# Which quads of the feed-forward blocks read stored weight sums, and when the sums are made

## The chip, the cores and the metric

The kernel runs on one core of a Trainium2 chip. The metric is the device time of one execution in microseconds, as the median of several runs.

## The reference

Two layers, each a token mixer and a feed-forward network, over 256 tokens of width 2048 in float32. The change touches the feed-forward part, whose work is

```python
def _swiglu(x, w_gate, w_up, w_down):
    h = jax.nn.silu(jnp.einsum('bsd,df->bsf', x, w_gate)) * jnp.einsum('bsd,df->bsf', x, w_up)
    return jnp.einsum('bsf,fd->bsd', h, w_down)

for i in range(DEPTH):
    mix = _hybrid_mixer(x, positions, w_in[i], g_cq[i], g_ckv[i], w_uq[i], w_ukv[i], w_o[i])
    x = _layer_norm(ALPHA * x + mix, ln1_g[i], ln1_b[i])
    ffn = _swiglu(x, w_gate[i], w_up[i], w_down[i])
    x = _layer_norm(ALPHA * x + ffn, ln2_g[i], ln2_b[i])
```

with a hidden width of 5632. The mixer projects x (`w_in`), runs a sparse attention and a latent attention (`w_uq`, `w_ukv`), and projects their outputs with `w_o`.

## The kernel before

**Units and remainders.** A weight tile (a unit) is 128x1024 float32, 512 KB: two k-tiles of 128 rows by 512 columns. SyncE's queue loads it into a tile `raw` (L323). `parts` (L338 to L351) splits it: ScalarE rounds it to `wh`, VectorE subtracts to get the remainder `wl`. TensorE computes a product with three matmuls of 128x512: x's high part with wh, with wl, and x's low part with wh. The tiles have a few buffers each (raw 4, wh and wl 5, and 6 and 2 more of them in the feed-forward part), so a load waits until the split of an earlier unit has read its buffer, and a split until the matmuls have read theirs.

**Blocks and quads.** The 5632 hidden columns are 11 blocks (`fc`, 0 to 10) of 512. Block 0 is computed plainly. For blocks 1 to 10, `gate_up` takes gate and up together, in four quads: quad u has the units u and u+4 of the 8 units of each matrix, which makes a 2x2 product (two token halves, two k halves, two matrices). There are three kinds. A *plain* quad (N) does the 8 products with 4 units. A *wino* quad (S) does 7 products with sums of weight units; it loads three units and, through GpSimd's queue, a sum of two (`load_sum`, L324 to L330: a load and an accumulating load), and VectorE makes three more sums in place (L1050, L1057, L1062) between the splits of its 7 units. A *made* quad (Q) has the same 7 products, but reads the four sums p4 to p7 ready from HBM, as plain loads of `raw`. A product is 6 matmuls. Per block the order of kinds is in `ORDER` and the quad of each in `UNIT` (L1150, L1151): block 1 is NSSS, blocks 2 and 3 SSNS, blocks 4 to 10 SSQS with u = 0 as the Q. VectorE adds the products up in `e` and `g` (L1032), ahead of `silu`.

**Operands.** The 7 products need sums of x's parts, too (`sum_operands`): av (L932), sv (L937), and their high and low parts in `few` or `many`. Those of quads 1 to 3 are made in block 0, those of quad 0 (`first_operands`, twelve VectorE instructions with the remainders of few at L396) in the down half ahead of block `ALLFROM` = 4, the first block that has a Q.

**Down halves.** From block 2 on, `down_half(fc)` ahead of each gate-and-up multiplies two earlier hidden blocks with half of `w_down`'s columns (L1105 to L1107).

**Stored sums.** `presums` (L770) is a generator that runs beside the attention: for each block from `ALLFROM` on, it loads four units into tiles q through GpSimd's queue (L778), which first writes one column from the newest wh, so that the load does not start earlier than that unit (L339); four units later a small GpSimd instruction (gate, L788) waits for the newest wh again, VectorE makes the four sums (L789 to L793), and GpSimd's queue stores them to HBM (L798). `spawn` starts a generator and each finished unit steps it (`tick`). `presums` is spawned behind the projection block TB and makes 7 sets in each layer; `finish(early)` ends it ahead of the output projection's last pass.

**Order.** The instructions of an engine stand in the order in which a scheduler puts the program; `high_priority` pulls some ahead. Each engine and each issuing queue works in its order and waits at the head for what it lacks. The mixer's blocks come as QI0, TA (the latents' block), QI1, TB, KA0 and so on; then `w_o` in four column blocks and a last pass (`last_pass`). `turn("more")` ahead of it closes the attention's pool of tiles and opens the pool of the feed-forward part: the first tile of the new pool waits for all that used the old memory, the stores of q among it.

Of the kernel before, what the change touches and what calls it, by code (L numbers as in the profile page):

```python
# [34 lines left out]
S = 256  # L35
# [26 lines left out]
SOON = 200  # L62
FIRSTD = 2
T2, T2MORE = 4, 6
ALLFROM, EARLY = 4, 0


QI0, TA, QI1, TB, KA0, QA0, VA0, KA1, QA1, VA1 = range(10)
# [14 lines left out]
def hybrid_trunk(ctx: ExitStack, tc: tile.TileContext, x, xt_in, pos, w_in, g_cq, g_ckv, w_uq,  # L83
# [28 lines left out]
    def pt(shape, dt, s, tag=None, bufs=1):  # L112
        assert phase["name"] == "att"
        return phase["pool"].tile(shape, dt, name=nm(s), tag=tag or s, bufs=bufs)
# [423 lines left out]
    def layer(l, xT, norms, last):  # L538
        xk = xlhs(xT)

        def in_chunk(b, before=None, split_t=None):
            n = IN_BLOCKS[b][1]
            return proj([(w_in[b][l, u], range(u * KU, (u + 1) * KU)) for u in range(NKT // KU)], xk, n,
                        before, split_t)
# [222 lines left out]

        ready = {}

        def presums():  # L770

            for fc in range(ALLFROM, NFC):
                u = EARLY

                def load(i, v):
                    d = pt([P, KU * C], F32, "q", bufs=4)
                    not_until_now(d)
                    nc.gpsimd.dma_start(d, w_gu[i][l, fc, v])  # L778
                    return d

                b12, b22 = load(1, u), load(1, u + HALF)
                yield 1
                b11 = load(0, u)
                yield 1
                b21 = load(0, u + HALF)
                yield 4
                gate = pt([P, 1], F32, "gate", bufs=2)
                nc.gpsimd.tensor_tensor(gate, b12[:, 0:1], f(latest["wh"][:, 0:1]), op=ALU.add)  # L788
                nc.vector.tensor_tensor(b12, b12, b22, op=ALU.add)  # L789
                nc.vector.tensor_tensor(b11, b12, b11, op=ALU.add)  # L790
                yield 1
                nc.vector.tensor_tensor(b22, b11, b22, op=ALU.subtract)
                nc.vector.tensor_tensor(b21, b11, b21, op=ALU.add)  # L793
                yield 1
                ready[fc] = {}
                for i, (name, v) in enumerate((("p7", b12), ("p6", b11), ("p5", b22), ("p4", b21))):
                    d = hbm.tile([P, KU * C], F32, name=nm("q"), tag=f"{l}_{fc}_{name}", bufs=1)
                    nc.gpsimd.dma_start(d, v)  # L798
                    ready[fc][name] = d
                    if i % 2:  # L800
                        yield 1
# [24 lines left out]
        ckvT = t4([P, 2, KVL // P, S], F32R, "ckvT")  # L826
        qpT = t4([P, M_HEADS // 2, S], F32, "qpT")
        bias = [pt([P, P * (t + 1)], F32, f"selb{t}") for t in range(NT)]
        o = in_chunk(TA)
        aff(1)  # L830
        p_ta = spawn(ta_post(o))
# [6 lines left out]
        p_tb = spawn(tb_post(o))  # L838
        if l == 0:
            load_x()  # L840
        early = spawn(presums())
        ka, p_ka = dsa_qk(KA0)
        finish(p_tb)
        o = proj([(w_uq[2][l, u], range(u * KU, (u + 1) * KU)) for u in range(QL // P // KU)], cqk, C)
# [54 lines left out]
                        nc.vector.scalar_tensor_tensor(sl, o, by, sl, op0=ALU.mult, op1=ALU.add)  # L899
                then(t)  # L900

        finish(early)
        turn("more")
        gbT = load_gbT(ln1_T[l])
        xT, norms = [], []
# [241 lines left out]
        def finish_hidden():  # L1147
            finish(*[h[2] for h in held])

        ORDER = {1: "NSSS", 2: "SSNS", 3: "SSNS"}  # L1150
        UNIT = {"NSSS": (0, 2, 3, 1), "SSNS": (1, 2, 0, 3), "SSQS": (1, 2, EARLY, 3)}  # L1151

        g = gu(0, 0, lambda: finish(*norms))
        affine(ln1_g[l], ln1_b[l], 0)
        u = gu(1, 0)
# [1 line left out]
        affine(ln1_g[l], ln1_b[l], 1)  # L1157
        spawn_hidden(0, g, u)
        for fc in range(1, NFC):
            order = ORDER.get(fc, "SSQS")  # L1160
            if fc >= FIRSTD:
                down_half(fc)
                finish_hidden()
            g, u = gate_up(fc, [({"N": "plain", "S": "wino", "Q": "made"}[k], v) for k, v in zip(order, UNIT[order])],
                           finish_hidden if fc < FIRSTD else None)
            if fc < FIRSTD:
                for c in range(2, D // C):
                    affine(ln1_g[l], ln1_b[l], c)
            spawn_hidden(fc, g, u)
# [69 lines left out]
```

## Time and profile before

| what | us |
|---|---|
| median of 3 runs (2143.92 to 2145.48) | 2145.45 |
| the profiled execution | 2147.09 |
| its span | 2145.3 |
| TensorE busy | 2129.4 (99%) |
| TensorE's weight loads busy | 1768.9 (82%) |
| VectorE busy | 1850.9 (86%) |
| ScalarE busy | 1311.5 (61%) |
| transfers | 260 GB/s on average |

The span runs from the first to the last instruction; the profiled execution's own time lies some 2 us above it. A busy TensorE is not one at its peak, since matmuls overlap: their starts tell its pace. Layer 1 repeats layer 0 some 1063.7 us later. The feed-forward blocks 1 to 4 of layer 0 lie between 434.78 and 661.05 us, each as a gate-and-up (to 475.69, 538.19, 600.28, 661.05) with a down half behind it. The granted TensorE clock is full in all the stretches below.

### The profile page before, as it was taken

What the parts mean: (1) busy time and instruction counts of PE and PEld (TensorE: products, weight loads), DVE (VectorE), ACT (ScalarE), POOL (GpSimd) and SP (SyncE); (2) the same over time, 40 slices, a digit from 0 to 9 for tenths busy, and PEclk for the clock granted to TensorE, in tenths of its full rate; (3) what the DMA queues carried; (4) which work ended last, traced back from release to release, by engine and by line L of the source; (5) the groups of instructions that cost most, each with busy time, mean ns of one, the idle gap of its engine ahead of it and who ended that gap; (6) DMA issues with size and microseconds to landing.
All of it is one profiled execution on the core that took longest, in us unless ns stands there. A gap on an engine that the chain in (4) does not pass through costs nothing.

```text
span 2145.3 us, 28442 instructions
## 1 busy us (share of the span) xinstructions
PE 2129.4 (99%) x9946; PEld 1768.9 (82%) x9946; DVE 1850.9 (86%) x2343; ACT 1311.5 (61%) x1695; POOL 321.6 (15%) x514
## 2 busy tenths in 40 slices
PE   9999999999999999999999999999999999999997
PEld 7888888888888888888888888888888888888886
DVE  6697776899999999999867976678999999999997
ACT  5555554766566666766655555447666666666773
POOL 0122220021111100110013222201111111110111
PEclk9999999999999999999999999999999999999999
DMA  8677879588888899888657877885897888989984
GB/s 295 216 279 272 310 277 328 175 217 267 239 245 270 286 278 300 269 273 255 216 176 242 298 276 276 315 281 187 245 274 224 256 265 274 288 275 293 286 296 115
DMA packets 161905, 558.21 MB, mean 260 GB/s; under 512 B 18161, under 2 KB 18465, under 8 KB 161121
## 3 DMA queue, kind: packets, MB, share of 16 engines
q1 hardware_dynamic: 111168, 399.69, 52.2%
q0 software_dynamic: 50448, 156.57, 28.4%
q8 instruction: 78, 1.28, 0.2%
q14 instruction: 67, 0.54, 0.1%
q10 hardware_dynamic: 144, 0.13, 0.0%
HBM read 503.37 MB, written 31.46 MB: 249 GB/s over the span
## 4 chain that ended last, share of the span: by engine, by line
PE 86%; DVE 7%; issue 3%; DMA 2%; ACT 1%; POOL 0%; SPq 0%; POOLq 0%; DVEq 0%; ACTq 0%
PE acc L372 8%; PE acc L373 8%; PE acc L374 8%; PE acc L1106 7%; PE acc L1107 7%; PE acc L1105 7%; PE gu_p L996 6%; PE gu_p L993 6%; PE gu_p L995 6%; DVE wl L351 3%; PE gu_c L993 3%; PE gu_c L996 3%; PE gu_c L995 3%; PE tr L392 2%; PE att L993 2%
## 5 line engine op out<-in xcount | busy, mean ns | idle before, releaser
L350 ACT ACTIVATE wh<-raw 128x1024 fp32r<-128x1024 f32 (+1 forms) x918 | 946.6, 1053 | 576.0 <-PE acc L374 142.8
L351 DVE TENSOR_TENSOR wl<-raw,wh 128x1024 fp32r<-128x1024 f32 (+1 forms) x918 | 1084.9, 1213 | 204.4 <-ACT wh L350 202.4
L372 PE MATMUL acc<-wh,xhl 128*128 128x512 f32 (+1 forms) x768 | 303.0, 395 | 0.8 <-ACT wh L350 0.7
L373 PE MATMUL acc<-wl,xhl 128*128 128x512 f32 (+1 forms) x768 | 297.2, 387 | 1.1 <-DVE wl L351 1.1
L374 PE MATMUL acc<-wh,xhl 128*128 128x512 f32 (+1 forms) x768 | 297.5, 388 | 0.0
L1105 PE MATMUL acc<-wh,hT 128*128 128x512 f32 x640 | 250.9, 392 | 0.0
L1106 PE MATMUL acc<-wl,hT 128*128 128x512 f32 x640 | 249.2, 389 | 0.1
L1107 PE MATMUL acc<-wh,hT 128*128 128x512 f32 x640 | 249.3, 390 | 0.0
L372 PEld LDWEIGHTS acc<-wh,xhl 128*128 128x128 f32 x768 | 144.7, 188 | 31.9 <-issue 3.9
L373 PEld LDWEIGHTS acc<-wl,xhl 128*128 128x128 f32 x768 | 144.8, 188 | 28.6 <-DVE wl L351 2.9
L374 PEld LDWEIGHTS acc<-wh,xhl 128*128 128x128 f32 x768 | 144.5, 188 | 27.9
L1106 PEld LDWEIGHTS acc<-wl,hT 128*128 128x128 f32 x640 | 120.2, 188 | 25.3 <-DVE wl L351 1.0
L1107 PEld LDWEIGHTS acc<-wh,hT 128*128 128x128 f32 x640 | 120.1, 188 | 25.1
L1105 PEld LDWEIGHTS acc<-wh,hT 128*128 128x128 f32 x640 | 120.2, 188 | 24.3
L1114 POOL DMA_DIRECT2D x<-d x80 | 67.8, 848 | 482.4 <-ACT d L1113 482.1
L995 PE MATMUL gu_c<-wl,xhl 128*128 128x512 f32 x344 | 134.0, 390 | 0.0
L996 PE MATMUL gu_c<-wh,xhl 128*128 128x512 f32 x344 | 133.8, 389 | 0.0
L993 PE MATMUL gu_c<-wh,xhl 128*128 128x512 f32 x344 | 133.8, 389 | 0.0
L993 PE MATMUL gu_p<-wh,many 128*128 128x512 f32 x240 | 93.4, 389 | 0.0
L995 PE MATMUL gu_p<-wl,many 128*128 128x512 f32 x240 | 93.4, 389 | 0.0
L996 PE MATMUL gu_p<-wh,many 128*128 128x512 f32 x240 | 93.4, 389 | 0.0
L1113 ACT ACTIVATE d<-acc 128x512 f32<-128x512 f32 x80 | 47.8, 597 | 71.5 <-PE acc L1107 70.8
(296 smaller groups left out, 3795.8 us busy)
## 6 DMA issues: line engine op xcount, KB each, us to landing
raw<-in_w_gate_dram SPq DMA_DIRECT2D x176, 512.0 KB, 5.4
raw<-in_w_down_dram SPq DMA_DIRECT2D x176, 512.0 KB, 8.6
raw<-in_w_in_dram SPq DMA_DIRECT2D x144, 512.0 KB, 5.2
sum<-in_w_up_dram POOLq DMA_DIRECT2D x120, 512.0 KB, 7.4
raw<-in_w_up_dram SPq DMA_DIRECT2D x102, 512.0 KB, 5.7
raw<-in_w_o_dram SPq DMA_DIRECT2D x64, 512.0 KB, 5.6
q<-q POOLq DMA_DIRECT2D x56, 512.0 KB, 4.4
raw<-q SPq DMA_DIRECT2D x56, 512.0 KB, 5.9
```

The costliest lines, as they stand in the source:

```text
L350: nc.scalar.activation(wh[:, :n], raw[:, :n], AF.Copy)
L351: nc.vector.tensor_tensor(wl[:, :n], raw[:, :n], f(wh[:, :n]), op=ALU.subtract)
L372: mm(o[t][:, :n], h, a, start=first, stop=False)
L373: mm(o[t][:, :n], h, b, start=False, stop=False)
L374: mm(o[t][:, :n], l, a, start=False, stop=final)
L993: mm(o[name], h, a, start=name not in begun, stop=False)
L995: mm(o[name], h, b, start=False, stop=False)
L996: mm(o[name], l, a, start=False, stop=end)
L1105: mm(o[c][t], h, wh[:, j, :], start=begin, stop=False)
L1106: mm(o[c][t], h, wl[:, j, :], start=False, stop=False)
L1107: mm(o[c][t], lo, wh[:, j, :], start=False, stop=end)
L1114: nc.gpsimd.dma_start(xt[t][:, c * C:(c + 1) * C], d, accum_op=ALU.add)
```

## The change

Blocks 1 to 4 and 6 to 10 get a made quad, block 5 none. Block 1 becomes NSQS, with quad 3 as the Q; blocks 2 and 3 become SSQS like 4 and 6 to 10; block 5 becomes SSSS. `presums` takes a list of (block, quad): 9 sets per layer, of which the first two, (1, 3) and (2, 0), are spawned right behind QI0 and the other seven behind TB as before, with a first wait of three units. `first_operands` moves from the down half ahead of block 4 to that ahead of block 2, with `ALLFROM` = 2.

```diff
-ALLFROM, EARLY = 4, 0
+ORDER = {1: "NSQS", 5: "SSSS"}
+UNIT = {"NSQS": (0, 2, 3, 1), "SSQS": (1, 2, 0, 3), "SSSS": (1, 2, 0, 3)}
+ALLFROM = 2
+
+
+def quads(fc):
+    order = ORDER.get(fc, "SSQS")
+    return list(zip(order, UNIT[order]))
...
-        def presums():
-
-            for fc in range(ALLFROM, NFC):
-                u = EARLY
+        made = [(fc, u) for fc in range(1, NFC) for k, u in quads(fc) if k == "Q"]
+
+        def presums(sets, wait=1):
+
+            yield wait
+            for fc, u in sets:
...
+        early = [spawn(presums(made[:2]))]
         o = in_chunk(TA)
...
-        early = spawn(presums())
+        early.append(spawn(presums(made[2:], 3)))
...
-        finish(early)
+        finish(*early)
...
-        ORDER = {1: "NSSS", 2: "SSNS", 3: "SSNS"}
-        UNIT = {"NSSS": (0, 2, 3, 1), "SSNS": (1, 2, 0, 3), "SSQS": (1, 2, EARLY, 3)}
```

Three places show how the order of instructions moves. The lines of the changed kernel are 10 to 13 higher than those of the kernel before: its L361 is L351, L406 is L396, L945 and L950 are L932 and L937, L977 is L964, L1045 is L1032, L1063, L1070 and L1075 are L1050, L1057 and L1062.

VectorE from block 1's last products into the down half behind it, before: remainders wl of the weights alternate with the adding up of the products in g and e.

```order
L1032 TENSOR_TENSOR e_4512<-e_4512,gu_p_4392 128x512
L351 TENSOR_TENSOR wl_4615<-raw_4612,wh_4614 128x1024
L1032 TENSOR_TENSOR g_4513<-gu_c_4271,e_4512 128x512
L351 TENSOR_TENSOR wl_4633<-raw_4630,wh_4632 128x1024
L1032 TENSOR_TENSOR e_4512<-e_4512,att_4296 128x1024
L351 TENSOR_TENSOR wl_4653<-raw_4650,wh_4652 128x1024
L1032 TENSOR_TENSOR e_4512<-e_4512,gu_p_4414 128x1024
L351 TENSOR_TENSOR wl_4685<-raw_4682,wh_4684 128x1024
L964 TENSOR_TENSOR g_4513<-g_4513,e_4512 128x1024
```

The same place in the changed kernel; wl_4669 and wl_4687 are the down half's first two remainders, wl_4732 its third.

```order
L361 TENSOR_TENSOR wl_4687<-raw_4684,wh_4686 128x1024
L1045 TENSOR_TENSOR e_4566<-e_4566,gu_p_4444 128x512
L406 TENSOR_TENSOR few_4704<-sv_4713,few_4704 128x256
L1045 TENSOR_TENSOR g_4567<-gu_c_4323,e_4566 128x512
L950 TENSOR_TENSOR sv_4717<-av_4702,av_4711 128x256
L1045 TENSOR_TENSOR e_4566<-e_4566,att_4348 128x1024
L945 TENSOR_TENSOR av_4721<-xhl_3751 128x256
L1045 TENSOR_TENSOR e_4566<-e_4566,gu_p_4466 128x1024
L406 TENSOR_TENSOR few_4704<-sv_4717,few_4704 128x256
L977 TENSOR_TENSOR g_4567<-g_4567,e_4566 128x1024
L950 TENSOR_TENSOR sv_4723<-av_4721,sv_4713 128x256
L361 TENSOR_TENSOR wl_4732<-raw_4729,wh_4731 128x1024
```

The down half's first two remainders now stand ahead of the adding up, and six small instructions of `first_operands` among it, ahead of the third remainder.

VectorE in block 5, from the second quad into the third, before: the third quad (raw_6528 to raw_6570, a Q) is seven remainders in a row.

```order
L351 TENSOR_TENSOR wl_6519<-raw_6453,wh_6518 128x1024
L351 TENSOR_TENSOR wl_6535<-raw_6528,wh_6534 128x1024
L351 TENSOR_TENSOR wl_6545<-raw_6530,wh_6544 128x1024
L351 TENSOR_TENSOR wl_6555<-raw_6532,wh_6554 128x1024
L351 TENSOR_TENSOR wl_6573<-raw_6564,wh_6572 128x1024
L351 TENSOR_TENSOR wl_6583<-raw_6566,wh_6582 128x1024
```

The same place in the changed kernel: the third quad is raw_6609 to raw_6613 with sum_6606.

```order
L361 TENSOR_TENSOR wl_6597<-raw_6531,wh_6596 128x1024
L361 TENSOR_TENSOR wl_6626<-raw_6611,wh_6625 128x1024
L361 TENSOR_TENSOR wl_6636<-raw_6613,wh_6635 128x1024
L1063 TENSOR_TENSOR raw_6609<-sum_6606,raw_6609 128x1024
L361 TENSOR_TENSOR wl_6658<-sum_6606,wh_6657 128x1024
L1070 TENSOR_TENSOR raw_6611<-raw_6609,raw_6611 128x1024
L361 TENSOR_TENSOR wl_6647<-raw_6609,wh_6646 128x1024
L1075 TENSOR_TENSOR raw_6613<-raw_6609,raw_6613 128x1024
```

Three sums now stand between its remainders.

TensorE at block 5's end, before: the last product (gu_p, three matmuls for each k-tile) and the first of the down half (acc).

```order
L993 MATMUL gu_p_6439<-wh_6692,many_4186 128x512
L995 MATMUL gu_p_6439<-wl_6693,many_4186 128x512
L996 MATMUL gu_p_6439<-wh_6692,many_4186 128x512
L993 MATMUL gu_p_6439<-wh_6692,many_4186 128x512
L995 MATMUL gu_p_6439<-wl_6693,many_4186 128x512
```

The same place in the changed kernel.

```order
L1006 MATMUL gu_p_6517<-wh_6768,many_4238 128x512
L1118 MATMUL acc_6783<-wh_6787,hT_6257 128x512
L1118 MATMUL acc_6821<-wh_6825,hT_6257 128x512
L1008 MATMUL gu_p_6517<-wl_6769,many_4238 128x512
L1009 MATMUL gu_p_6517<-wh_6768,many_4238 128x512
```

Two matmuls of the down half, which read no remainder, now stand ahead of the one that reads the last product's.

SyncE's queue at the end of the attention, before, with the semaphores waited for (DMASW are GpSimd's transfers, the stores of q among them; raw_3606, raw_3616 and raw_3621 are units of the last pass, the others of `w_o`'s column blocks).

```order
L323 DMA raw_3425<-in_w_o_dram 128x1024 [waits DMAHW7_49,DVE_49]
L323 DMA raw_3606<-in_w_o_dram 128x1024 [waits DMASW3_49,DMASW2_49,DMASW4_49,DMASW1_49,DMASW5_49,DMASW0_49,DMASW6_49,PE_49,DMASW7_49,Activation_49,Pool_49]
L323 DMA raw_3443<-in_w_o_dram 128x1024 [waits DMAHW0_49,DVE_49]
L323 DMA raw_3616<-in_w_o_dram 128x1024
L323 DMA raw_3621<-in_w_o_dram 128x1024
L323 DMA raw_3461<-in_w_o_dram 128x1024 [waits DMAHW1_49,DVE_49]
```

The same place in the changed kernel; raw_3495 and raw_3513 are the units of raw_3443 and raw_3461.

```order
L333 DMA raw_3495<-in_w_o_dram 128x1024 [waits DMAHW0_49,DVE_49]
L333 DMA raw_3658<-in_w_o_dram 128x1024 [waits DMASW3_49,DMASW4_49,DMASW2_49,DMASW5_49,DMASW1_49,DMASW6_49,DMASW0_49,DMASW7_49,PE_49,Pool_49]
L333 DMA raw_3513<-in_w_o_dram 128x1024 [waits DMAHW1_49,DVE_49]
L333 DMA raw_3668<-in_w_o_dram 128x1024
L333 DMA raw_3535<-in_w_o_dram 128x1024 [waits DMAHW2_49,DVE_49]
```

The load that waits for the old pool's transfers stands one unit later, and two last-pass units that stood ahead of raw_3461 stand behind raw_3513.

## Rows read from the trace of the kernel before

**Rows 1.** The page: busy shares by engine, and the chain that ended last.

```profile
PE 2129.4 (99%) x9946; PEld 1768.9 (82%) x9946; DVE 1850.9 (86%) x2343; ACT 1311.5 (61%) x1695; POOL 321.6 (15%) x514
PE 86%; DVE 7%; issue 3%; DMA 2%; ACT 1%; POOL 0%; SPq 0%; POOLq 0%; DVEq 0%; ACTq 0%
```

**Rows 2.** Stretches: length, busy us and instructions by engine, clock, transfers' share, GB/s.

```profile
434.78:475.69 40.91, 40.83 (x184) 33.26 (x182) 39.80 (x43) 25.83 (x28) 9.38 (x12) 1.00 0.84 216
475.69:498.75 23.06, 23.00 (x106) 18.77 (x104) 22.95 (x23) 13.13 (x16) 2.51 (x4) 1.00 0.86 262
498.75:538.19 39.44, 39.44 (x176) 32.66 (x174) 36.27 (x34) 27.30 (x28) 5.06 (x7) 1.00 0.94 276
538.19:560.84 22.65, 22.65 (x105) 18.84 (x104) 20.29 (x20) 11.64 (x14) 2.54 (x4) 1.00 0.69 213
...
661.05:683.70 22.65, 22.65 (x105) 18.85 (x104) 21.64 (x21) 11.45 (x14) 2.51 (x4) 1.00 0.83 252
683.70:721.78 38.08, 38.08 (x169) 31.54 (x168) 36.19 (x34) 28.51 (x31) 5.05 (x7) 1.00 0.91 294
...
1686.65:1724.73 38.08, 38.08 (x169) 31.53 (x168) 36.19 (x34) 28.52 (x31) 5.23 (x7) 1.00 0.92 291
```

**Rows 3.** The chain in order of time, later in layer 0: start, us, what.

```profile
384.49 0.44 PE tr L392 x4
```

**Rows 4.** TensorE's instructions at block 1's end: start, us, instruction [idle before].

```profile
473.93 0.39 PE L993 MATMUL gu_p<-wh,few 128*128 128x512 f32 x1
474.40 0.50 PE L995 MATMUL gu_p<-wl,few 128*128 128x512 f32 x1
```

**Rows 5.** VectorE's instructions at block 1's end.

```profile
473.14 1.21 DVE L351 TENSOR_TENSOR wl<-raw,wh 128x1024 fp32r<-128x1024 f32 x1
```

**Rows 6.** VectorE's instructions in block 5.

```profile
703.83 5.76 DVE L351 TENSOR_TENSOR wl<-raw,wh 128x1024 fp32r<-128x1024 f32 x5
...
718.82 1.21 DVE L351 TENSOR_TENSOR wl<-raw,wh 128x1024 fp32r<-128x1024 f32 x1
```

**Rows 7.** TensorE's instructions in block 5 and the down half behind it.

```profile
715.21 0.39 PE L995 MATMUL att<-wl,many 128*128 128x512 f32 x1
...
722.01 0.39 PE L1106 MATMUL acc<-wl,hT 128*128 128x512 f32 x1
```

**Rows 8.** VectorE's waits from 622.97 to 683.7 us: total us, times, longest.

```profile
DVE wl L351 <- ACT wh L350: 2.8, 2, 1.9
```

**Rows 9.** VectorE's instructions of the first operands, at block 3's end.

```profile
590.57 0.41 DVE L932 TENSOR_TENSOR av<-xhl 128x256 f32<-128x256 f32 x1
...
593.41 0.75 DVE L396 TENSOR_TENSOR few<-sv,few 128x256 fp32r<-128x256 f32 x2
```

**Rows 10.** Stretches of the attention.

```profile
40.00:60.00 20.00, 20.00 (x94) 16.65 (x93) 10.15 (x22) 9.57 (x13) 0.00 (x0) 1.00 0.86 317
...
320.00:340.00 20.00, 20.00 (x92) 16.68 (x91) 10.10 (x10) 7.69 (x8) 2.81 (x4) 1.00 1.02 335
```

**Rows 11.** GpSimd's instructions: the last set's gate and its last store.

```profile
303.65 1.22 POOL L788 TENSOR_TENSOR gate<-q,wh 128x1 f32<-128x1 f32 x1 [10.21 <-ACT wh L350]
...
314.29 0.53 POOL L798 DMA_DIRECT2D q<-q  x1 [1.78 <-DVE q L793]
```

**Rows 12.** ScalarE's instructions there.

```profile
313.95 1.06 ACT L350 ACTIVATE wh<-raw 128x1024 fp32r<-128x1024 f32 x1 [0.92 <-PE acc L374]
```

**Rows 13.** DMA issues from 300 to 360 us: count, KB each, median us to landing.

```profile
q<-q POOLq DMA_DIRECT2D x4, 512.0 KB, 4.0
```

**Rows 14.** SyncE's queue: the first loads into the next pool.

```profile
321.50 2.29 SPq L323 DMA_DIRECT2D raw<-in_w_o_dram  x4
```

**Rows 15.** The chain in order of time from 320 to 400 us.

```profile
329.53 0.33 SPq L323
329.91 12.89 DMA raw<-in_w_o_dram
```

**Rows 16.** TensorE's instructions at the wait behind it.

```profile
346.33 0.50 PE L373 MATMUL acc<-wl,oA 128*128 128x512 f32 x1 [0.25 <-DVE wl L351]
```

More of the change, by code (lines that the diff above doesn't have):

```diff
@@ L1159, in layer @@
         for fc in range(1, NFC):
-            order = ORDER.get(fc, "SSQS")
             if fc >= FIRSTD:
@@ L1163, in layer @@
                 finish_hidden()
-            g, u = gate_up(fc, [({"N": "plain", "S": "wino", "Q": "made"}[k], v) for k, v in zip(order, UNIT[order])],
+            g, u = gate_up(fc, [({"N": "plain", "S": "wino", "Q": "made"}[k], v) for k, v in quads(fc)],
                            finish_hidden if fc < FIRSTD else None)
```

## The prediction

> **What bounds the kernel now.** I read the busy shares first, then the chain that ended last, then the table of stretches of the feed-forward blocks, then the instructions at their edges. TensorE is busy for 99% of the span, and the chain of waits runs over it for 86%, over VectorE for 7%, over transfers for 2% [rows 1]. Time can leave in two ways only: fewer matmuls, or fewer moments at which one waits.
>
> The stretches show the first. Block 2's gate-and-up, with a plain quad, lasts 39.44 us; block 5's, with three summed quads and a stored one, 38.08, in layer 1 too; a down half lasts 22.65 [rows 2].
>
> Block 1 shows the second. Its gate-and-up has the same products as block 2's and eight transposes more (184 instructions to 176), at 0.44 us for four [rows 3]. 39.44 + 0.88 + 22.65 = 62.97, and 40.91 + 23.06 = 63.97 are measured. The missing **1.0 us** are waits like this one: matmuls start every 0.227 us, but the one at 474.40 starts 0.47 behind its forerunner [rows 4]. It reads a weight remainder (wl) that VectorE began at 473.14 and ended at 474.35 [rows 5]. Of VectorE's 128x1024 instructions one lasts 1.22 us, but the next begins before that: five in a row take 5.76 [rows 6], so (5.76 − 1.22) / 4 = 1.135 each.
>
> So I keep a second book, the **lead**: the time from the end of a remainder to the first matmul that reads it. In block 1 it is near zero. In block 5 the last of those five remainders ends at 709.59 and is read at 715.21; the one begun at 718.82 ends at 720.03 and is read at 722.01 [rows 6, 7]: **1.98 us** are left at the end of the gate-and-up. VectorE is busy there for 36.19 of 38.08 us, and for 21.64 of 22.65 in a down half [rows 2]. It idles only where it has run so far ahead that ScalarE has no free buffer to convert into, 2.8 us in a block's period [rows 8]; that is early in the gate-and-up, so what is added behind it comes out of the 1.98.
>
> **The change part by part.**
>
> *Blocks 2 and 3, the plain quad made from stored sums.* Each loses 39.44 − 38.08 = 1.36 us, six matmuls of 0.227; two blocks in two layers: **−5.44 us**. VectorE gets three remainders more in each, 3.41 us. Block 2's period had 36.27 + 20.29 = 56.56 busy [rows 2]; 59.97 of then 60.73 still fits, by less than 1 us. I take no stall; bound 1 per layer.
>
> Weight loads keep TensorE busy for only 82% of the span [rows 1], and for 32.66 us of block 2's 39.44 and 31.54 of block 5's 38.08, which is the same share. The Trainium skill (Perfetto Trace Analysis, Identifying the Most-Contended Engine) calls matmul busy time a poor measure of how full TensorE is, and weight-load share a good one; by it a sixth of TensorE would be free, and six matmuls fewer need return nothing. The two blocks disagree with that: the whole 1.36 us came back.
>
> *Block 1, one summed quad made from stored sums, and the first operands early.* Seven products either way. VectorE loses three sums (3.41 us) and gets twelve small instructions that ran about the end of block 3: four av, four sv, four remainders of few. At 0.41 us alone and 0.34 behind one another [rows 9] they are 4.1 to 4.9 us; I take 4.6, net +1.2. In the order six of them stand early in the block, where there is lead, and six in the down half behind it, with the products' sums e and g, all ahead of its third remainder. Carried through with these durations, the waits at block 1's end go and that third remainder comes 1.0 to 1.2 us late. The stall moves by some 10 us and keeps its size: **+0.2 us** for both layers; bounds −2.0 (it vanishes) and +2.4 (1.2 on top, twice).
>
> *Block 4* is rid of the twelve. It did not wait for VectorE: zero.
>
> *Block 5, the stored quad summed.* Matmuls as before. VectorE gets three sums, 3.41 us, in a gate-and-up that ended with 1.98 to spare: 1.98 − 3.41 = −1.43. TensorE's new order has one or two matmuls with ready weights pulled into the gap, worth 0.1 to 0.4; I take a wait of 1.3 per layer, **+2.6 us**. Bounds: 0, if e and g fall behind the remainders that are waited for, and 4.0, if the fourth sum load in a row is late as well. Block 1 has three in a row now, and VectorE was idle for no more than 1.1 us there (39.80 of 40.91, rows 2).
>
> *Two sets ahead of the latents' block.* Per layer 8 additions on VectorE (9.1 us), 8 loads and 8 stores of 512 KB. From 40 to 60 us VectorE is busy for 10.15 of 20 and the transfers' share is 0.86 [rows 10]: the additions fit, and only they wait for the loads. Zero; bound 1 per layer.
>
> *The seven later sets end later.* The gate of the last one waits for the unit converted just ahead of 303.65 [rows 11]; in the new order it stands behind the unit whose conversion ended at 315.01 [rows 12], 11.4 us on. The last store, issued at 314.29 [rows 11], so comes at 325.7 and lands 4.0 later [rows 13], at 329.7. SyncE's queue holds a load into a buffer of the next pool, which waits for these landings; it was issued at 321.50 [rows 14], and the output projection's loads stand behind it. Transfers are full here, a share of 1.02 from 320 to 340 us [rows 10]: a load of this projection that went out at 329.53, when VectorE had freed its buffer, took 12.89 us [rows 15], and TensorE idled before the matmul at 346.33 that reads its remainder [rows 16]. In the new order that load has one last-pass load ahead of it instead of three, 1 MB less, some 3 us at 335 GB/s; but 2 MB of stores come into the full stretch. Issued at 329.7, just as now, and with 10 to 13 us in flight, it is there at 340 to 343; the loads behind it have some us of lead. I take 0.5 us in layer 0 and 0.2 in layer 1: **+0.7**. Bounds −0.8 (the present wait goes, twice) and +8 (4 us per layer, by a landing at 347).
>
> *The sum:* −5.44 + 0.2 + 2.6 + 0.7 = **−1.9 us**. The profiled execution took 2147.09 us around its span of 2145.3, which is 1.64 above the median of 2145.45. Against its own time the forecast is 2145.2, against the median **2143.5**.
>
> **The rivals.**
>
> *No VectorE stall* (faster). The order lets the remainders that are waited for go first in block 5, and block 1's stall goes too. For it: the program rearranges TensorE's and VectorE's order at just these places. Against it: VectorE has next to no idle time into which work could move. −5.44 − 2.0 = −7.4: 2138.0; with block 1's stall kept, 2140.0.
>
> *The end of the attention stalls* (slower). The late sets' last store lands at 334 or later and the pool's first load holds SyncE's queue; with 12.9 us of flight, as now, the projection's load lands at 347, and from there each further microsecond is one of TensorE. For it: transfers are full, and one matmul waits as it is. Against it: fewer last-pass bytes stand ahead of that load. At 338 in both layers, 4 to 5 us each on top of the other parts' −2.6: 2151 to 2153.
>
> *Nothing is left* (same). Blocks 1 and 5 at their upper ends, 2.4 + 4.0, eat the 5.44 and 0.7 stays: 2146.4 to 2147.1.
>
> *Six matmuls fewer return nothing* (same), since TensorE's weight loads or something behind them hold the pace: 0 + 0.2 + 2.6 + 0.7 = +3.5, so 2149.0. Blocks 2 and 5 of the present kernel speak against it. This is the rule of the Trainium skill's Perfetto Trace Analysis above.
>
> **How the numbers follow.** A measurement of this kernel tells about 0.2%, 4.3 us, from no change: faster is below 2141.2, slower above 2149.7. The forecast case (the gain partly given back, 2141.5 to 2146) has 0.47, nothing left 0.14, no VectorE stall 0.22, the attention's end 0.15, of which 0.01 ends short of 2149.7, matmuls that return nothing 0.02. Faster 0.22, same 0.64, slower 0.14. The range takes in most of the faster case and the near part of the slower one, where one layer stalls: 2138.5 to 2150.0. All lower bounds together, −5.44 − 2.0 − 0.8, would be 2137.2, all upper ones over 2156; both need every part at its end.
>
> **What would show it.** Blocks 2 and 3: a gate-and-up of 38.08 instead of 39.44; if not, the first term is wrong. Block 5: some 39.4 instead of 38.08, with a matmul that waits for a remainder at its last quad; 38.1 would make the forecast too slow, 41 too fast. Block 1: 40.3, and a down half behind it longer than 23.06. At the attention's end: the last store of q at about 326 us, the first load of the next pool at about 330, and gaps of TensorE under 1 us; a gap of 4 there would be the slower rival.

## The result: 26 us slower

The changed kernel takes **2171.01 us** (median of 4 runs, 2168.08 to 2177.99), the kernel before 2144.94 (4 runs): a ratio of 1.0126, interval 1.0108 to 1.0145. The forecast was 2143.5, range 2138.5 to 2150.0. The profiled execution took 2171.02 with a span of 2169.2, 23.9 us more than the span of before.

The page tells that it is not TensorE's work that grew: with 24 matmuls fewer it is busy for 2131.9 us, 2.5 more than in [rows 1]. Its share of the chain fell from 86 to 78%, that of transfers rose from 2 to 6% and that of "issue" from 3 to 5.

```profile
span 2169.2 us, 28581 instructions
PE 2131.9 (98%) x9922; PEld 1768.6 (82%) x9922; DVE 1882.1 (87%) x2371; ACT 1320.7 (61%) x1707; POOL 346.5 (16%) x566
PE 78%; DVE 8%; DMA 6%; issue 5%; ACT 1%; POOL 1%; POOLq 0%; SPq 0%; DVEq 0%; ACTq 0%
```

Where the time went is read by putting the start of the same matmul in both traces side by side (the first matmul of a weight unit or of a block). The difference grows only where time is lost:

```
matmul                            before    after   difference  in the stage
layer 0, unit of QI0               24.52    21.20      -3.3       -3.3
  before TA's operands             58.08    54.77      -3.3        0.0
  behind them                      66.49    68.94      +2.5       +5.8
  output projection, late         348.96   350.76      +1.8       -0.7
  block 0                         388.34   396.86      +8.5       +6.7
  block 1                         434.78   443.30      +8.5        0.0
  block 2                         498.75   506.98      +8.2       -0.3
  block 3                         560.84   567.73      +6.9       -1.3
  block 5                         683.70   689.23      +5.5       -1.4
  block 6                         744.47   751.44      +7.0       +1.4
layer 1, unit of TA              1118.61  1125.64      +7.0        0.0
  four units on                  1129.76  1147.10     +17.3      +10.3
  behind QI1                     1151.57  1168.90     +17.3        0.0
  in TB                          1184.89  1208.00     +23.1       +5.8
  output projection, late        1425.87  1448.60     +22.7       -0.4
  last units                     1455.36  1480.39     +25.0       +2.3
  block 1                        1498.45  1523.48     +25.0        0.0
  block 2                        1562.43  1587.26     +24.8       -0.2
  block 3                        1624.53  1647.99     +23.5       -1.4
  block 5                        1747.39  1769.49     +22.1       -1.4
  block 6                        1808.15  1832.28     +24.1       +2.0
```

The −3.3 at the start is not the change: the kernel before, profiled, had waits of 0.6, 0.9 and 1.0 us there and matmuls at a lower clock behind them (a granted clock of 0.83 from 10 to 20 us), and in the experiments below, whose code is the same at that point, this figure lies between −1.8 and −3.7. Differences of whole profiles to that one, which took 2147.09 us, are therefore some 2 us smaller than those of the medians; the stages behind the start are not touched by it. The rest has three parts. The feed-forward part **gains** 1.5 us in layer 0 and 0.9 in layer 1. The starts of the attention **lose** 5.8 and 16.1 us, its ends 6.7 and 2.3.

**The feed-forward part** in the table of stretches (blocks 1, its down half, 2 and 3, and block 5 with its down half), to be read against [rows 2]:

```profile
443.30:483.63 40.33, 40.33 (x183) 33.49 (x182) 39.63 (x47) 28.34 (x31) 7.99 (x10) 1.00 0.86 252
483.63:506.98 23.35, 22.98 (x105) 18.83 (x104) 23.32 (x27) 12.48 (x17) 2.39 (x4) 1.00 0.80 244
506.98:545.06 38.08, 38.08 (x169) 31.53 (x168) 37.49 (x36) 30.03 (x31) 5.19 (x7) 1.00 0.94 303
567.73:605.81 38.08, 38.08 (x169) 31.53 (x168) 36.19 (x34) 28.53 (x31) 5.32 (x7) 1.00 0.92 287
689.23:751.44 62.21, 61.60 (x274) 50.15 (x272) 59.82 (x56) 40.84 (x45) 8.66 (x12) 1.00 0.87 248
```

Blocks 2 and 3 take 38.08 instead of 39.44. Block 1 lost its waits (40.33), its down half got some (23.35). Block 5 with its down half takes 62.21 instead of 38.08 + 22.69 = 60.77.

**Layer 0's start.** TensorE stops at the transposes behind TA, and what follows runs at the lower of its two clock levels, 1.2 GHz: matmuls start 0.43 us apart, not 0.227, and the granted clock from 60 to 70 us is 0.83.

```profile
61.70 0.30 PE L402 MATMUL tr<-ident,dup 128*128 128x128 f32 x1 [3.93 <-DVE dup L584]
...
62.67 0.63 PE L382 MATMUL acc<-wh,xhl 128*128 128x512 f32 x1
63.10 0.63 PE L383 MATMUL acc<-wl,xhl 128*128 128x512 f32 x1
```

The chain in order of time leads from there back to VectorE's rotation of those operands (dup), which stands in its order behind a weight remainder, and that waited for a weight load that was 12.39 us under way:

```profile
46.01 12.39 DMA raw<-in_w_in_dram
...
58.51 1.06 ACT wh L360
59.57 0.02 issue
59.59 1.22 DVE wl L361
```

In the stretches the transfers are full from 40 to 60 us, a share of 1.00 at 390 GB/s, where it was 0.86 at 317 [rows 10]:

```profile
40.00:60.00 20.00, 17.77 (x79) 14.40 (x77) 10.81 (x18) 7.07 (x11) 4.67 (x11) 1.00 1.00 390
60.00:70.00 10.00, 8.30 (x30) 6.75 (x31) 5.16 (x10) 4.83 (x8) 1.43 (x2) 0.83 0.91 360
```

Among the DMA issues from 40 to 60 us (count, KB each, median us to landing) the weights take 12.4 us, the early sets' stores 12.7, and one of the two loads of x, which the output projection needs, 12.9. Before (first line) the weights took 5.0:

```profile
raw<-in_w_in_dram SPq DMA_DIRECT2D x6, 512.0 KB, 5.0
...
raw<-in_w_in_dram SPq DMA_DIRECT2D x5, 512.0 KB, 12.4
q<-q POOLq DMA_DIRECT2D x4, 512.0 KB, 12.7
x<-in_x_dram SPq DMA_DIRECT2D x1, 1024.0 KB, 12.9
```

**Layer 1's start.** Layer 1 loads no x, but its affine runs here: g and b of the last norm, by GpSimd's queue, and multiplications by g on VectorE. The early sets are in the same queue (instructions of GpSimd, VectorE and TensorE).

```profile
1113.72 1.77 POOL L464 DMA_DIRECT2D x<-in_ln_b_dram  x2 [6.67 <-DVE x L463]
1115.26 0.80 POOL L790 DMA_DIRECT2D q<-in_w_gate_dram  x1
1115.83 0.52 POOL L800 TENSOR_TENSOR gate<-q,wh 128x1 f32<-128x1 f32 x1
1116.29 0.58 POOL L461 DMA_DIRECT2D g<-in_ln_g_dram  x1
...
1126.05 0.69 DVE L463 TENSOR_TENSOR x<-x,g 128x512 f32<-128x512 f32 x1 [7.19 <-DMA g<-in_ln_g_dram]
...
1130.80 0.80 PE L383 MATMUL acc<-wl,xhl 128*128 128x512 f32 x1 [4.78 <-DVE wl L361]
1131.40 0.63 PE L384 MATMUL acc<-wh,xhl 128*128 128x512 f32 x1
```

Read upwards: TensorE waits 4.78 us for a remainder; VectorE makes it late, since it stood 7.19 us in front of a multiplication by a g that had not landed; that g was issued at 1116.29, behind a set's load and gate and behind a bias load that waited 6.67 us for VectorE. Before, VectorE came to the same multiplication without a wait:

```profile
1103.44 1.28 DVE L453 TENSOR_TENSOR x<-x,g 128x512 f32<-128x512 f32 x2
```

**The end of layer 0's attention.** The last gate and the last store (compare [rows 11]), and TensorE's waits behind them:

```profile
317.51 1.22 POOL L800 TENSOR_TENSOR gate<-q,wh 128x1 f32<-128x1 f32 x1 [10.99 <-ACT wh L360]
...
324.95 0.53 POOL L810 DMA_DIRECT2D q<-q  x1 [0.60 <-DVE q L805]
...
356.76 0.80 PE L382 MATMUL acc<-wh,oB 128*128 128x512 f32 x1 [3.12 <-ACT wh L360]
358.20 0.80 PE L383 MATMUL acc<-wl,oB 128*128 128x512 f32 x1 [0.65 <-DVE wl L361]
```

The chain in order of time tells what lies between. The store takes 7.79 us to land, and SyncE's queue, which issued its last load at 325.8, stands until then; at 333 five loads and two sums go out within 2 us. The split of these units comes late, and so does the freeing of their buffers: the load that TensorE waits for goes out at 343.23, right behind one that had no buffer until 342.86, and takes 11.44 us.

```profile
324.95 7.79 DMA q<-q
...
333.01 3.93 DMA raw<-in_w_o_dram
...
342.86 0.33 SPq L333
343.18 0.05 issue
343.23 11.44 DMA raw<-in_w_o_dram
354.70 1.06 ACT wh L360
```

Behind the waits nine matmuls run at 1.2 GHz (granted clock 0.79 from 350 to 360 us), 0.2 us too long each: with gaps of 3.3, 1.2 and 0.4 us that makes the 6.7.

### The profile page after: what moved, and what is told of

Read it like the earlier page. It is cut to its first block, busy times and chain, and to the rows that moved or that the text cites. A ratio compares the mean times of both kernels' runs of the same rounds, so it can differ in the third digit from the quotient of the medians.

```text
span 2169.2 us, 28581 instructions
## 1 busy us (share of the span) xinstructions
PE 2131.9 (98%) x9922; PEld 1768.6 (82%) x9922; DVE 1882.1 (87%) x2371; ACT 1320.7 (61%) x1707; POOL 346.5 (16%) x566
## 4 chain that ended last, share of the span: by engine, by line
PE 78%; DVE 8%; DMA 6%; issue 5%; ACT 1%; POOL 1%; POOLq 0%; SPq 0%; DVEq 0%; ACTq 0%
PE acc L1119 7%; PE acc L1120 7%; PE acc L1118 6%; PE acc L382 6%; PE acc L383 6%; PE acc L384 6%; PE gu_p L1008 6%; PE gu_p L1009 6%; PE gu_p L1006 6%; DVE wl L361 4%; PE gu_c L1008 3%; PE gu_c L1009 3%; PE gu_c L1006 3%; PE tr L402 2%; DMA raw<-in_w_in_dram 2%
## 5 line engine op out<-in xcount | busy, mean ns | idle before, releaser
L360 ACT ACTIVATE wh<-raw 128x1024 fp32r<-128x1024 f32 (+1 forms) x930 | 956.4, 1053 | 566.1 <-PE acc L384 135.2
L361 DVE TENSOR_TENSOR wl<-raw,wh 128x1024 fp32r<-128x1024 f32 (+1 forms) x930 | 1099.8, 1215 | 171.5 <-ACT wh L360 169.9
L1008 PE MATMUL gu_c<-wl,xhl 128*128 128x512 f32 x328 | 127.7, 389 | 0.6 <-DVE wl L361 0.6
L1006 PE MATMUL gu_c<-wh,xhl 128*128 128x512 f32 x328 | 127.7, 389 | 0.4 <-ACT wh L360 0.4
L1009 PE MATMUL gu_c<-wh,xhl 128*128 128x512 f32 x328 | 127.6, 389 | 0.0
L339 POOL DMA_DIRECT2D sum<-in_w_up_dram x60 | 33.3, 555 | 411.4 <-DVE wl L361 389.4
L1009 PE MATMUL gu_p<-wh,many 128*128 128x512 f32 x240 | 93.4, 389 | 0.0
```

The costliest lines, as they stand in the source:

```text
L360: nc.scalar.activation(wh[:, :n], raw[:, :n], AF.Copy)
L361: nc.vector.tensor_tensor(wl[:, :n], raw[:, :n], f(wh[:, :n]), op=ALU.subtract)
L1006: mm(o[name], h, a, start=name not in begun, stop=False)
L1008: mm(o[name], h, b, start=False, stop=False)
L1009: mm(o[name], l, a, start=False, stop=end)
```

## The experiments

My theory after the result had three causes: transfers (too many bytes from 40 to 62 us of layer 0 and about 1155 to 1185 of layer 1), GpSimd's queue (layer 1 at 1120), and three units of delay (the ends). Its rivals were the feed-forward part and transfers that are full whatever the sets' place. Differences below are, as in the table, to the profiled execution of before, stage by stage.

**No first wait.** The seven later sets stand at the units where they stood before; the early ones stay.

```diff
-            yield wait
+            if wait:
+                yield wait
...
-        early.append(spawn(presums(made[2:], 3)))
+        early.append(spawn(presums(made[2:], 0)))
```

> The changed kernel with no first wait of three units ahead of the seven later sets, so that they stand at the same units as in the kernel before; the two early sets stay. Theory: at the attention's end the changed kernel loses 6.7 us in layer 0 (unit of 349 us to unit of 363) and 2.3 in layer 1 because the last stores land at 332.7 us and the next pool's first load, which waits for them, holds SyncE's queue. With the sets three units (some 8 us) earlier these losses fall under 1 us each, and the time to 2171 - 8 = 2163 (2161 to 2165). Rival, that the transfers are full there whatever the sets' place: the losses stay and the time is 2169 to 2171. The losses in the first third of each layer stay with both (5.7 and 16 us).

2164.99 us, 1.0092 (1.0077 to 1.0107). The end of layer 0 lost 1.2 us between 287 and 388 us of before (4.2 to 5.4), where the changed kernel lost 6.2, that of layer 1 nothing (21.3 to 21.0). The last store went out at 318.48 us; less the 4.2 us that this run was behind, that is the 314.29 of before [rows 11]. The starts lost 6.2 and 17.7 us, somewhat more than the 5.8 and 16.1 of the changed kernel's profile. So all but some 1 of the ends' 9 us belong to the three units, in a kernel with the early sets.

**The three units alone**, in the kernel before:

```diff
         def presums():
 
+            yield 3
             for fc in range(ALLFROM, NFC):
```

> The kernel before with a first wait of three units ahead of its seven sets, nothing else. Theory, that these three units alone cost the attention's ends, without any early set: the stores of the last set land some 8 to 11 us later, the next pool's first load holds SyncE's queue, and layer 0 loses 5 to 8 us and layer 1 1 to 3 between the output projection's last units: 2151 to 2155. Rival, that it takes the two early sets as well: 2145 to 2147.

2156.77 us, 1.0057 (1.0042 to 1.0071): 12 us for one line, more than forecast. Layer 0 lost 6.5 us with the same picture, a wait of 3.60 and slow matmuls behind it:

```profile
320.04 0.53 POOL L799 DMA_DIRECT2D q<-q  x1 [0.60 <-DVE q L794]
329.27 1.06 POOL L329 DMA_DIRECT2D sum<-in_w_up_dram  x2 [8.70 <-PE acc L374]
...
352.35 0.50 PE L372 MATMUL acc<-wh,oB 128*128 128x512 f32 x1 [3.60 <-ACT wh L350]
354.39 0.63 PE L374 MATMUL acc<-wh,oB 128*128 128x512 f32 x1
354.82 0.63 PE L372 MATMUL acc<-wh,oB 128*128 128x512 f32 x1
```

Layer 1 lost 6.4 us with it, between the units of 1350.9 and 1425.9 of before, where the changed kernel lost nothing; that kernel's 2.3 came behind them. The chain leads over a load that was 17.41 us under way in this kernel and over one of 12.44 in the changed one; why they differ is open. That it is the stores' landing that costs, and not the later place of the last additions, is read from the chain; no run parts the two.

**No early sets.** The attention's sets as before; seven of them feed blocks 3, 4 and 6 to 10.

```diff
-ORDER = {1: "NSQS", 5: "SSSS"}
+ORDER = {1: "NSSS", 2: "SSNS", 5: "SSSS"}
...
-ALLFROM = 2
+ALLFROM = 3
...
-        early = [spawn(presums(made[:2]))]
+        early = []
...
-        early.append(spawn(presums(made[2:], 3)))
+        early.append(spawn(presums(made, 0)))
```

> The seven sets stand at the same places of the attention as in the kernel before, no set ahead of the latents' block; blocks 3, 4 and 6 to 10 read them (block 1 NSSS, block 2 SSNS, block 5 SSSS), and the first operands are made ahead of block 3. Theory, that all the loss comes from the place and number of the sets in the attention: the attention takes what it took before, block 3 gains 1.36 us, block 5 loses 1.4 to 2.0, per layer; total 2145 to 2147. Rival, that the feed-forward part with these kinds loses by itself: 2150 or more.

2145.38 us, 1.0005 (0.9996 to 1.0015): the kernel before. Its attention is that of before (the difference moves by under 0.4 us in either layer), block 3 gains 1.36 in each layer, block 5 loses 1.75 and 1.91. The stretches of block 3's gate-and-up and of block 5 with its down half:

```profile
557.99:596.07 38.08, 38.08 (x169) 31.53 (x168) 36.19 (x34) 28.74 (x31) 5.04 (x7) 1.00 0.95 292
679.49:742.01 62.52, 61.66 (x273) 50.22 (x272) 60.53 (x58) 40.56 (x45) 9.00 (x13) 1.00 0.88 249
```

So a stored set that moves from block 5 to block 3 is worth nothing here: what the missing matmuls give, the fourth quad of sums takes.

**Layer 1's gains by SyncE's queue.**

```diff
-    def affine(g, b, c):
+    def affine(g, b, c, queue=None):
...
-        nc.gpsimd.dma_start(gc, g[sl].partition_broadcast(P))
+        (queue or nc.gpsimd).dma_start(gc, g[sl].partition_broadcast(P))
...
-                affine(ln2_g[l - 1], ln2_b[l - 1], c)
+                affine(ln2_g[l - 1], ln2_b[l - 1], c, nc.sync)
```

> The changed kernel with the gains g of layer 1's affine loaded by SyncE's queue instead of GpSimd's; nothing else. In the changed kernel VectorE stands 7.2 us at the multiplication by g from 1118.9 us, since that load is issued at 1116.3 behind the set's loads and a bias load that waits for VectorE in GpSimd's queue; TensorE then waits 4.9 us. Theory, that the order of GpSimd's queue is the cause: the wait at 1130.8 goes, the loss of 10.3 us between the units of 1121 and 1127 falls to 4 or less, total 2163 to 2166. Rival, that the transfer engines' load is the cause: g lands late all the same, the loss stays within 2 us of 10.3, total 2169 to 2172. Layer 0 is not touched and loses as before.

2164.07 us, 1.0093 (1.0076 to 1.0110). The loss of 10.3 us fell to 1.4. This g went out at 1105.12 us instead of 1116.29; VectorE waits 1.86 us for it instead of 7.19 and has the next remainders made in time:

```profile
1112.80 0.69 DVE L463 TENSOR_TENSOR x<-x,g 128x512 f32<-128x512 f32 x1 [1.86 <-DMA g<-in_ln_g_dram]
...
1114.54 0.69 DVE L463 TENSOR_TENSOR x<-x,g 128x512 f32<-128x512 f32 x1
...
1116.71 1.22 DVE L361 TENSOR_TENSOR wl<-raw,wh 128x1024 fp32r<-128x1024 f32 x1
```

The set's loads, sums and stores are all still there. It was the order of GpSimd's queue, not the bytes. The later loss, about 1160 to 1185, stayed at 5.4. VectorE stands in front of a g there too, the last of the four: 5.22 us in the changed kernel, where it was issued behind the second set's stores, and 6.28 in this one, where it is in SyncE's queue:

```profile
1160.16 0.55 POOL L461 DMA_DIRECT2D g<-in_ln_g_dram  x1
1169.63 1.29 DVE L463 TENSOR_TENSOR x<-x,g 128x512 f32<-128x512 f32 x2 [5.22 <-DMA g<-in_ln_g_dram]
...
1160.27 1.29 DVE L463 TENSOR_TENSOR x<-x,g 128x512 f32<-128x512 f32 x2 [6.28 <-DMA g<-in_ln_g_dram]
```

**No stores of the early sets.** They are loaded and added up, but blocks 1 and 2 read weight units in place of the stored sums, so this kernel's result leaves those sums out.

```diff
+                    if wait == 1:
+                        ready[fc][name] = w_gu[i % 2][l, fc, u + HALF * (i // 2)]
+                        continue
                     nc.gpsimd.dma_start(d, v)
                     ready[fc][name] = d
```

> The changed kernel whose two early sets are loaded and added up, but not stored; blocks 1 and 2 read weight units of the same size in place of the stored sums (so that part of the result is not the reference's; times of these blocks stay comparable). Theory, that the loss in layer 0 at 60 us is one of transfers (8 loads, 8 stores and x of 2 MB in a stretch at 410 to 420 GB/s, weights landing 12 to 14 us after their issue): without the stores the weights issued at 46 to 54 us land in 6 to 8 us, the wait of 4.1 us at 61.7 goes and so does the slow clock behind it, slip 1 us or less instead of 5.7. In layer 1 the queue's part stays: 6 to 12 of 16 us. Total 2158 to 2166. Rival, that the additions on VectorE or the loads alone make the wait: the wait at 61.7 stays at 3 to 4 us, total 2168 or more.

2163.07 us, 1.0091 (1.0074 to 1.0108). Layer 0's start loses 0.6 us instead of 5.8, and layer 1's later loss, 5.8, is gone too (from 1152 to 1185 the difference falls by 0.4). Layer 1's 10.7 at 1120 stay, as the queue's share should. So both other losses hang on the stores; VectorE's additions were in this kernel and cost layer 0 the 0.6 at most. Whether the stores cost by their bytes, the next run tells for layer 0. For layer 1 no run parts their bytes from the last g's wait: without the stores VectorE came to that multiplication without a wait, so both went together.

**x loaded late.** The two loads of x stand ahead of the output projection.

```diff
         p_tb = spawn(tb_post(o))
-        if l == 0:
-            load_x()
...
+        if l == 0:
+            load_x()
         first = [8, 10, 12, 14, 0, 2]
```

> The changed kernel with the two loads of x (2 MB, needed only at the output projection) issued ahead of that projection instead of at 39 to 43 us; nothing else. Theory, that in layer 0 too many bytes meet between 40 and 62 us: 2 MB less leave the loss of 5.7 us there at 2 or less, total 2165 to 2168. Rival, that the early sets' own 16 transfers are enough for it: 4 us or more stay, total 2169 to 2172. Layer 1 has no such load and loses as before.

2168.28 us, 1.0108 (1.0093 to 1.0123). The loads of x go out at 215.6 and 220.7 us. Layer 0's start loses **nothing** (−1.8 ahead of it and behind it), with both sets' 16 transfers in place. Its stretch from 40 to 60 us is still full:

```profile
40.00:60.00 20.00, 20.00 (x91) 16.51 (x91) 15.60 (x26) 10.07 (x15) 9.43 (x13) 1.00 0.99 371
```

But its DMA issues there tell of weights that land in 7.0 us and stores that land in 6.6. In the kernel without the stores (last line) the weights took 9.1:

```profile
raw<-in_w_in_dram SPq DMA_DIRECT2D x6, 512.0 KB, 7.0
q<-q POOLq DMA_DIRECT2D x4, 512.0 KB, 6.6
...
raw<-in_w_in_dram SPq DMA_DIRECT2D x6, 512.0 KB, 9.1
```

Either 2 MB of x or the stores could be there, not both. The total fell by less than the 5.8, since the end of layer 0 lost more here, 8.4 instead of 6.7 (what made it longer is open), and the start was 1.5 us slower than in the changed kernel's profile.

The x goes by SyncE's queue, the stores by GpSimd's, and either slows the weights. The Trainium skill (DMA: Bandwidth & Descriptors, Issuing engines are not separate DMA queues) says that transfers run on the same 16 engines and interleave whichever engine issued them; the runs agree: weights in 12.4 us with both there, in 7.0 without x, in 9.1 without the stores.

**All three together.**

> The changed kernel with three things undone or moved together: no first wait ahead of the later sets, layer 1's gains by SyncE's queue, x loaded late. Theory, that the losses are separate and add up: the attention's ends lose 1 us or less each, layer 0's start 2 or less, layer 1's start 6 to 7 (what its transfers alone cost when the gains went by SyncE), the feed-forward part gains 2.4: 2148 to 2152. Rival, that a relieved place hands its bytes to the next one: 2155 or more.

2151.9 us, 1.0032 (1.0020 to 1.0043). Layer 0 loses nothing at its start and nothing at its end, and its feed-forward part gains 1.5: there the change does what the sum said. In layer 1 that part gains 0.5, and the end loses nothing. Its start still loses 7.2 (1.7 at 1120, 5.5 at 1155 to 1180), with the transfers full and the clock down behind a wait. The chain to that wait leads from TensorE over ScalarE to a weight load that went out late, behind VectorE's multiplication by the last g, and that g was 7.45 us under way:

```profile
1139.62 7.45 DMA g<-in_ln_g_dram
...
1155.00:1165.00 10.00, 8.07 (x37) 6.71 (x36) 7.22 (x16) 6.28 (x14) 2.85 (x4) 0.83 1.03 411
```

In layer 0 the stretch from 40 to 60 us moves 392 GB/s, as much as the changed kernel's 390, and TensorE does not stop; the weights land in 7.0 us:

```profile
40.00:60.00 20.00, 20.00 (x91) 16.54 (x90) 14.23 (x26) 10.88 (x16) 8.15 (x12) 1.00 1.01 392
...
raw<-in_w_in_dram SPq DMA_DIRECT2D x5, 512.0 KB, 7.0
```

The losses add up within what was expected; a place relieved did not load the next. The profiled execution was the fastest of the six, 2148.91 us: where the other 3.0 us of the median lie, no trace shows.

**Eight sets**, one of them early, for blocks 3 to 10, with gains and x moved as above; then the same with the early set eight units later.

```diff
-ORDER = {1: "NSQS", 5: "SSSS"}
+ORDER = {1: "NSSS", 2: "SSNS"}
...
-ALLFROM = 2
+ALLFROM = 3
...
-        early = [spawn(presums(made[:2]))]
+        early = [spawn(presums(made[:1]))]
...
-        early.append(spawn(presums(made[2:], 3)))
+        early.append(spawn(presums(made[1:], 0)))
```

> Eight sets per layer, one ahead of the latents' block at the place of the changed kernel's first one, seven at the places of the kernel before; blocks 3 to 10 read them (block 1 NSSS, block 2 SSNS), gains by SyncE and x late. Theory, that half the early transfers fit: the starts lose 1 us or less in layer 0 and 1 to 3 in layer 1, the ends nothing, block 3 gains 1.36 per layer and no block has four sums to make: 2142 to 2146. Rival, that already one early set's stores collide with the weights: 2148 or more.

> As the kernel with eight sets, but the early set waits for eight units, so that its stores come at some 60 to 66 us in layer 0, where the kernel before has a transfer share of 0.50 (60 to 80 us). Theory: nothing is lost in layer 0, under 2 us in layer 1; 2141 to 2144. Rival, that the early set costs wherever it stands: as the kernel with eight sets, or more.

2143.87 us, 0.9996 (0.9987 to 1.0005), and 2144.24 us, 0.9997 (0.9988 to 1.0006). The early set is free in layer 0 in both. In layer 1 it costs 2.2 at 1120 and 0.7 up to 1185; set back by eight units, 3.8 at 1160 to 1185. The second half of the theory, that a better place in layer 1 costs under 2 us, fell.

**Eight or nine sets in layer 0 alone**; layer 1 has the seven sets, kinds and places of before.

```diff
+ORDER = ({1: "NSSS", 2: "SSNS"}, {1: "NSSS", 2: "SSNS", 3: "SSNS"})
...
+ALLFROM = (3, 4)
...
+        ne = (0 if l else 1)
+        early = [spawn(presums(made[:ne]))] if ne else []
...
+        early.append(spawn(presums(made[ne:], 0)))
```

> Layer 0 as in the kernel with eight sets (gains by SyncE and x late), layer 1 with the seven sets, kinds and places of the kernel before. Theory, that the early set costs nothing in layer 0 and 2.9 us in layer 1: as the kernel with eight sets less 1 to 1.5 us, 2142 to 2143.5. Rival, that what layer 1 lost there was drift of another cause: no better than 2143.9.

> As the last, but with nine sets in layer 0, two of them ahead of the latents' block; blocks 2 to 10 read them, block 1 stays NSSS, first operands ahead of block 2. Theory, that two early sets cost nothing in layer 0 with x late: block 2 gains another 1.36 us, against which the first operands add up to 2 us of waits of TensorE behind block 1, which has three quads to sum and no lead: 2141.5 to 2144.

Eight: **2142.73 us, 0.9989 (0.9979 to 0.9998)**, the only version whose interval lies below 1, by about 2 us. Layer 1 then loses nothing at its start. The profile is that of its slowest execution, 2144.78 us; there layer 0 lost 0.7 us at its start and 1.3 at its end. Nine: 2143.12 us, 0.9996 (0.9987 to 1.0004). From block 1 to block 3 of layer 0 the difference grew by 0.5 us although block 2 had six matmuls fewer: by the starts of its matmuls TensorE lost 0.4 and 0.9 us at the two longest waits of block 1's down half. So the first operands, which fall there, took the ninth set's gain. Layer 0's start, with two sets ahead, lost nothing. The difference between the two versions is below what these runs can tell.

## Why the prediction was wrong

*Blocks 2 and 3, −5.44.* Right to the hundredth: 38.08 instead of 39.44, in both layers. The rule of the Trainium skill that was weighed there (Perfetto Trace Analysis, Identifying the Most-Contended Engine) would have let six matmuls fewer return nothing; they returned all.

*Block 1 and the first operands, +0.2.* Measured −0.3 and −0.2, with the mechanism told: the gate-and-up 40.33 for 40.3 told, the down half 23.35 instead of 23.06.

*Block 5, +2.6.* Measured 1.4 and 2.0, so +3.5, and 1.75 and 1.91 without early sets, with the wait told, for a remainder at the last quad (725.83 us, 0.61 idle). The lead's bare account, 1.98 − 3.41 = −1.43, was nearer than the 1.3 that I took on account of the matmuls pulled into the gap. The feed-forward terms came to −2.6 by forecast and −2.5 by measurement; part of that is luck, since block 1 was 0.7 better than told and block 5 0.9 worse. (The row of layer 1 in [rows 2] is block 4's, which has the same kinds as block 5 had.)

*Two sets ahead of the latents' block: zero, bound 1 per layer.* **This step failed**: 5.8 us in layer 0, 16.1 in layer 1. I had seen the share of 0.86 from 40 to 60 us, asked where the additions fit and who waits for the set's own loads, and stopped. The question not asked was what the set's transfers do to *others*. The stretches would have answered it: 4 stores and 3 loads of 512 KB are 3.7 MB in these 20 us, 180 GB/s beside the 317 that were there, and no such stretch of before moves more than 360. (Without the 2 MB of x, which are 105 GB/s of it, the sum is 396, and that fitted: the runs with two early sets and x late moved 371 to 392 there.) In layer 1 I took the stretch for a copy of layer 0's. It isn't: the affine's loads stand in GpSimd's queue there, and a set put ahead of them delays a VectorE instruction at the head of its queue. The trace of before shows the affine at 1096 to 1146 us; my rows came from layer 0.

*The later sets, +0.7, and the slower rival.* The mechanism was told, its date too: less the 2.35 us that this execution was behind there, the last store went out at 322.6 for 325.7 told and landed at 330.4 for 329.7 (two errors that cancel: it took 7.8 us, not the 4.0 of stores with room around them). The size was off, 9.0 instead of 0.7, and the rival's 8 to 10 was the truth at a date at which I had not let it decide, 330 instead of 334. **The step that failed** is "the loads behind it have some us of lead". I followed the one load behind the barrier, which was indeed in time, and not the next ones: they wait for a buffer that a late unit has to free, the second goes out at 343.2 and takes its 11 us on top. The present kernel has the same pair, and I read it as one: in [rows 15] the load of 12.89 us went out at 329.91, behind another one issued at 329.53. A delay ahead of a full stretch is handed on from buffer to buffer.

*Left out of every price:* the clock. The waits at 61.7 and at 356.8 us were followed by matmuls at 1.2 GHz, which cost 1.6 and 1.8 us on top of the waits themselves.

*The rivals.* No VectorE stall: no, block 5 waited as told. Nothing left, six matmuls that return nothing: no.

## What to carry to other kernels

A transfer that nobody waits for still has a price: before work is moved into a stretch, add its bytes to what the stretch moves already, and look at the landing times of the loads that the bound engine waits for. Look at the stretch in every layer, since queues are shared by other work in each; and ask of a queue not only what the moved instruction waits for but what stands behind it. Where a pool's first tile waits for the last user of the old memory, the last transfer's landing, under the load that is there then, is the date to work with: three units of delay cost 12 us here.

## What the runs showed of the hardware

From 40 to 60 us, loads of 512 KB landed in 5.0 us (median) before, at 317 GB/s, in 7.0 to 8.8 with x late, at 371 to 392, and in 12.4 in the changed kernel, at 390. So the rate of a stretch that is full does not tell how long a load is under way: at 335 GB/s and a share of 1.02, one took 12.89 us in the kernel before [rows 10, 15].

After a wait of TensorE of 3.9 us (61.7), 4.8 (1130.8) and 3.1 (356.8), matmuls started 0.43 us apart for some 3 to 4 us. Behind shorter waits it went either way: they did behind 1.9 us (1139.9) and the 1.7 at 1194.3, and did not behind 0.6 (725.8), 1.6 (1459.2) and the 1.7 at 1173.0, with a granted clock of 1.00.
